# One decoder block with sixteen experts: a shorter routing step, a first expert gathered in quarters, and a norm row built later

## The chip, the cores and the metric

The kernel runs on one core of a Trainium2 chip. The metric is device time in microseconds (us) of one execution of the whole kernel. Lower is better.

## The reference, cut to what matters

256 tokens of width 2048 go through a mixing layer (8 attention heads, 8 gated recurrent heads, one output projection with a residual) and then through a mixture of experts: each token picks one of 4 groups and the 2 best of the 4 experts in it. All matrices are float32.

```python
x = x + jnp.concatenate([o_attn, o_rec], -1) @ w_out          # mixing layer
h2 = rms_norm(x, norm_ffn_g)
grp_w, grp_idx = lax.top_k(softmax(h2 @ w_grp + b_grp), 1)     # one group of 4
exp_logits = (h2 @ w_er[group] + b_er[group])                  # 4 experts in it
top_w, top_idx = lax.top_k(softmax(exp_logits), 2)             # two of them
combine = one_hot(4 * grp_idx + top_idx) * top_w / sum(top_w) * grp_w
for each expert e:
    hid = silu(h2 @ w_gate[e]) * (h2 @ w_up[e]) * combine[:, e]
    out = out + hid @ w_down[e]
return rms_norm(x + out, final_norm_g)
```

Each expert has 3 x 2048 x 1024 float32 weights, 25.2 MB. Sixteen of them are 403 MB and all are read.

## The kernel before

**Front half.** `proj_t` and `proj_n` run the projections on TensorE (PE). Weights come through two 1 MB buffers, are split into a high and a low part by ACT (L298) and DVE (L299) in units of half a buffer (`units`), and 24 matmuls per unit use them. After each unit `step(k)` lets the queue `bgq` of background generators go on by k steps. The last projection is by `w_out`, over two halves of its rows. The second half goes in five column blocks b = 0 to 4, the last two 256 wide (2 units each). After each block `out_block` adds to the residual `X` (= `x2`), squares it for the norm, transposes it, copies it to `xT` or `rd`, and adds its part of the router logits into `pl` (L679).

**Routing.** After `drain()` the logits `pl` are copied (L703), folded and turned to tokens on partitions by two matmuls into `plt` (L706), scaled by the row norm `r2` and biased into `Z` (L714). `first_max` finds the maximum of four and the first place that holds it, in five DVE operations. It runs for the best expert and the group together and again for the second expert. `selb` is the selection (L742). Five small matmuls (L744 to L748) give each token its rank in its expert, `rk`. `keep_busy` (L699) puts matmuls of no use into the gaps of PE.

**Experts.** Each expert takes up to 64 tokens (`CAP`). `gather_matrix` makes a 0/1 matrix `pg` scaled by `r2`. `gather` multiplies it with `x2` (16 matmuls of 512 columns, tile `pn`), ACT copies to `xn`, and `turn` transposes eight times and multiplies by the norm gain into `xg`, 16 chunks of 128 rows. For expert e, PE then runs in a fixed order (`mmo` and `transpose` keep program order): the gate product `ga` over four weight pieces, with `scatter` of expert e - 1 after the first piece, the up product `up` over four pieces, `gather` for e + 1, the transposes of `hid`, `turn` for e + 1, and the down product `pd` over four pieces. `gather` covers the time in which ACT and DVE make `hid`. At e = 1, after the third gate piece, `final_gain` builds a row of the last norm with 16 matmuls that have 16 rows.

**Weights of the experts.** All loads are issued by SP in one order. A piece is 2 MB. Pieces are numbered through: expert 0 has 0 to 11 (gate 0 to 3, up 4 to 7, down 8 to 11), expert 1 has 12 to 23, and so on. Pieces 0 to 10 are loaded before the experts start (0 in two halves, its second half last, into the buffer of the last split weights). The ring has nine buffers. From piece 21 on, piece p goes into the buffer of piece p - 9, so its load waits until PE has used that piece. Pieces 12 to 20 take over those of pieces 1 to 6 and 8 to 10, and the halves of 11 those of the halves of 0. So piece 22 (a down piece of expert 1) waits for 13 (a gate piece of expert 1), piece 24 (expert 2) for 15, and piece 29 for 20.

Of the kernel before, what the change touches and what calls it, by code (L numbers as in the profile page):

```python
# [9 lines left out]
F32 = mybir.dt.float32  # L10
# [9 lines left out]
P = 128  # L20
T = 256
NT = 2
# [15 lines left out]
def hybrid_block_kernel(  # L38
# [141 lines left out]
    rev = cst.tile([P, 4], F32, name="rev")  # L180
    nc.gpsimd.iota(rev, pattern=[[-1, 4]], base=4, channel_multiplier=0,
                   allow_small_or_imprecise_dtypes=True)

    ssq = cst.tile([P, NT, 5], F32, name="ssq")
    small8 = cst.tile([P, 8], F32, name="small8")
# [150 lines left out]
    def proj_n(aTh, aTl, c0=0, c1=NC, w=512):  # L336

        pp = pbig().rearrange("p (n f) -> p n f", n=2)[:, :, 0:w]
        c = c0
        while c < c1:  # L340
            for hi, lo in units():
                for k in range(1024 // w):
                    for n in range(NT):
                        ts = slice(n * P, (n + 1) * P)
                        ah, al = aTh[c // 8][:, c % 8, ts], aTl[c // 8][:, c % 8, ts]
                        mm(pp[:, n], ah, hi[:, k], start=c == c0, stop=False)  # L346
                        mm(pp[:, n], ah, lo[:, k], start=False, stop=False)  # L347
                        mm(pp[:, n], al, hi[:, k], start=False, stop=c == c1 - 1)  # L348
                    c += 1
                step(2 if c0 else 1)  # L350
        return pp


# [299 lines left out]
    pl = pm.tile([64, T], F32, name="pl")  # L653
    x2 = X

    def out_block(b, col, w, pp, last):
        bs = slice(col, col + w)
        for n in range(NT):
            V.tensor_tensor(x2[:, n, bs], x2[:, n, bs], pp[:, n], ALU.add)
            if last:  # L660
                jk = cst.tile([P, 512], BF16, name="jk", tag="jk", bufs=1)
                S.activation(jk[:, 0:w], x2[:, n, bs], AF.Square, accum_out=ssq[:, n, b:b + 1])
        yield
        if not last:
            return
        k = w // P
        for j in range(0, k, 2):
            xT = xTs[xi[0] % 2]
            xi[0] += 1
            pt = psmall().rearrange("p (j t) -> p j t", j=2)  # L670
            for i in range(2):
                for n in range(NT):
                    nc.tensor.transpose(
                        pt[:, i, n * P:(n + 1) * P],
                        x2[:, n, bs].rearrange("p (q j) -> p j q", j=k)[:, j + i], ident)
            V.tensor_copy(xT, pt)
            yield
            for i in range(2):
                mm(pl[32 * i:32 * i + 32], wr[:, col // P + j + i], xT[:, i],  # L679
                   start=b == 0 and j == 0, stop=b == 4)  # L680
            yield

    xTs = [cm.tile([P, 2, T], F32, name="xT"), rd]
# [1 line left out]
    for hf, blocks in ((0, half0), (1, half1)):  # L685
        for b, (col, w) in enumerate(blocks):
            pp = proj_n(oTh, oTl, 8 * hf, 8 * hf + 8, w)
            bgq.append(out_block(b, col, w, pp, hf == 1))
        if hf == 0:
            S.activation(rf[:, 0:1], rf[:, 0:1], AF.Sqrt)  # L690
    drain()
    while nxt < NEARLY:
        load()
# [2 lines left out]

    def keep_busy(k, ps, lhs, rhs):
        for i in range(k):
            mm(ps[0:lhs.shape[1], 0:P], lhs, rhs, start=True, stop=True)  # L699

    keep_busy(8, busy, ident, x2[:, 1, D - P:])
    lt = dist1[0:64]
    V.tensor_copy(lt, pl)  # L703
    plt = psmall()[:, :40].rearrange("p (n e) -> p n e", n=NT)
    for n in range(NT):
        mm(plt[:, n], lt[:, n * P:(n + 1) * P], fold[0:64], start=True, stop=True)  # L706


    r2 = small8[:, 2:4]
# [1 line left out]
    rstd(r2, r2, D)  # L711
    Z = cst.tile([P, 5, NT, 4], F32, name="Z")
    for n in range(NT):
        V.scalar_tensor_tensor(Z[:, :, n], plt[:, n].rearrange("p (g e) -> p g e", g=5),  # L714
                               r2[:, n:n + 1], bias.rearrange("p (g e) -> p g e", g=5),
                               ALU.mult, ALU.add)

    def first_max(dst, src, m, tmp, vm, k):

        V.tensor_reduce(m, src, AX.X, ALU.max)  # L720
        V.tensor_tensor(tmp, src, m.unsqueeze(2).to_broadcast([P, k, 4]), ALU.is_equal)
        V.tensor_tensor(tmp, tmp, rev.unsqueeze(1).to_broadcast([P, k, 4]), ALU.mult)
        V.tensor_reduce(vm, tmp, AX.X, ALU.max)
        V.tensor_tensor(dst, tmp, vm.unsqueeze(2).to_broadcast([P, k, 4]), ALU.is_equal)

    Zf = Z.rearrange("p g n e -> p (g n) e")
    ma = cst.tile([P, 10], F32, name="ma")
    mb = cst.tile([P, 8], F32, name="mb")
    vm = cst.tile([P, 10], F32, name="vm")
    tmp = cst.tile([P, 10, 4], F32, name="tmp")  # L730
    M1 = cst.tile([P, 10, 4], F32, name="M1")
    M2 = cst.tile([P, 8, 4], F32, name="M2")
    E2 = cst.tile([P, 8, 4], F32, name="E2")
    keep_busy(8, busy, Z.rearrange("p g n e -> p (g n e)"), ident)
    first_max(M1, Zf, ma, tmp, vm, 10)
    keep_busy(6, busy, M1.rearrange("p a e -> p (a e)"), ident)
    V.scalar_tensor_tensor(E2, M1[:, 0:8], -1e30, Zf[:, 0:8], ALU.mult, ALU.add)
    first_max(M2, E2, mb, tmp[:, 0:8], vm[:, 0:8], 8)
    V.tensor_tensor(M2, M2, M1[:, 0:8], ALU.add)
    gm = M1[:, 8:10].rearrange("p n g -> p g n").unsqueeze(3).to_broadcast([P, 4, NT, 4])  # L740
    selb = cst.tile([P, 4, NT, 4], BF16, name="selb")
    V.tensor_tensor(selb, M2.rearrange("p (g n) e -> p g n e", g=4), gm, ALU.mult)  # L742
    pr = psmall()[:, :48].rearrange("p (a g e) -> p a g e", a=3, g=4)
    mm(pr[:, 0], before, selb[:, :, 0], start=True, stop=True)  # L744
    mm(pr[:, 1], ones, selb[:, :, 0], start=True, stop=False)
    mm(pr[:, 1], before, selb[:, :, 1], start=False, stop=True)
    mm(pr[:, 2], ones, selb[:, :, 0], start=True, stop=False)
    mm(pr[:, 2], ones, selb[:, :, 1], start=False, stop=True)  # L748
# [6 lines left out]
    V.tensor_reduce(cmax, pr[:, 2].rearrange("p g e -> p (g e)"), AX.X, ALU.max)  # L755

# [5 lines left out]
    over = cst.tile([P, NT, 4, 4], F32, name="over")  # L762
    cmaxi = cst.tile([1, 1], I32, name="cmaxi")

    def weights_of_routes():
        V.tensor_tensor(Zf, Zf, ma.unsqueeze(2).to_broadcast([P, 10, 4]), ALU.subtract)
# [6 lines left out]
        V.tensor_tensor(tmp[:, 8:10], Zf[:, 8:10], M1[:, 8:10], ALU.mult)  # L773
# [9 lines left out]
        V.tensor_copy(cmaxi, cmax[:1])  # L783

    cm.release()
    pm.release()
    mp = tc.alloc_tile_pool(name="mp", bufs=1, side="right")
# [6 lines left out]
    def piece(e, kind, i):  # L794
        return loaded.pop((e * 3 + kind) * 4 + i)


    def mmo(*a, **k):
        tc.keep_in_program_order(mm(*a, **k))  # L799

    def transpose(dst, src):
        tc.keep_in_program_order(nc.tensor.transpose(dst, src, ident))  # L802

    def pscr():
        return pq.tile([P, 512], F32, name="pt", tag="pt", bufs=2)
# [25 lines left out]
    def turn(xn):  # L831

        xg = mp.tile([P, NC, CAP], F32, name="xg")
        for j in range(2):
# [4 lines left out]
            for z in range(2):  # L839
# [2 lines left out]
                                gfe[:, c0:c0 + 4].unsqueeze(2).to_broadcast([P, 4, CAP]),  # L842
                                ALU.mult)
        return xg

    def scatter_matrix(e):
        pcm = mp.tile([P, NT, P], F32, name="pcm")
# [49 lines left out]
            S.activation(gf[:, q * 512:(q + 1) * 512], ps.rearrange("p c f -> p (c f)"), AF.Copy)  # L897
        return gf

    xg = turn(gather(gather_matrix(0)))  # L900
    weights_of_routes()
    pend = None
    work = None
    for e in range(NE):
        ga = pq.tile([P, 512], F32, name="ga")
        up = pq.tile([P, 512], F32, name="up")
        for i in stream(ga, xg, e, 0):
            if i == 0 and pend is not None:
                if e == 1:
                    acc[1] = single(0, [P, D], name="acc1")  # L910
                scatter(*pend)
            if i == 2 and e == 1:
                gf = final_gain()
        for i in stream(up, xg, e, 1):
            if i == 1:
# [20 lines left out]
        if e + 1 < NE:  # L936
            xg = turn(xn)
        pd = ptwo("pd")
        if e < NE - 1:
# [160 lines left out]
```

## Time and profile before

| | |
|---|---|
| median of 3 runs | 1420.9 us (1419.77 to 1421.42) |
| the profiled execution | 1423.41 us, its span 1421.6 us |
| PE | 1324.4 us busy, 93% |
| DVE, ACT | 432.2 us, 275.1 us |
| read from memory | 480.54 MB |
| chain that ended last | PE 67%, DMA 29%, DVE 2%, ACT 1% |

The front half runs to about 480 us, the routing and the first gather to about 496 us, the experts to about 1409 us. The rows of the trace that are used below count from the start of the span. PE is TensorE's matmuls, DVE VectorE, ACT ScalarE, SPq the sequencer that issues DMAs. A granted clock of 1.00 is 2.4 GHz and 0.50 is 1.2 GHz.

### The profile page before, as it was taken

The numbers are of one execution on the slowest core, as the hardware profiler recorded it, in microseconds if no ns is written. First come the engines' busy times: TensorE is split into PE (matmuls) and PEld (weight loads), VectorE is DVE, ScalarE is ACT, GpSimd is POOL, SyncE is SP. The second block draws the span as 40 slices with busy tenths as digits, with TensorE's granted clock in tenths as the row PEclk, the third lists the DMA queues.
The fourth block names the chain that finished last, engine by engine and source line by source line (L and its number), as shares of the span: only waits on it lengthen the run. The fifth ranks groups of instructions, "written<-read, shape, count | busy, mean of one in ns | idle before, by whom it ended". The sixth has DMA issues, their size and how long they took to land.

```text
span 1421.6 us, 16461 instructions
## 1 busy us (share of the span) xinstructions
PE 1324.4 (93%) x7073; PEld 721.8 (51%) x7073; DVE 432.2 (30%) x646; ACT 275.1 (19%) x408; POOL 17.8 (1%) x47
## 2 busy tenths in 40 slices
PE   7999999999999999999999999898898988989885
PEld 7999898898887733333333323223232232322323
DVE  4554557557555411112112112111121111211112
ACT  5453543532533300000000000000000000000002
POOL 2000000000000000000000000000000000000002
PEclk9999999999999999999999999999999999999998
DMA  6555553554598598999999999999999999999995
GB/s 235 210 181 169 163 177 119 178 178 178 212 345 300 208 405 364 389 427 429 428 427 428 427 429 428 427 427 427 428 429 427 428 427 428 428 428 427 427 411 207
DMA packets 85437, 483.75 MB, mean 340 GB/s; under 512 B 16816, under 2 KB 19056, under 8 KB 60528
## 3 DMA queue, kind: packets, MB, share of 16 engines
q1 hardware_dynamic: 84704, 482.61, 84.1%
q8 instruction: 57, 0.93, 0.3%
q14 instruction: 20, 0.16, 0.0%
q10 hardware_dynamic: 656, 0.04, 0.0%
HBM read 480.54 MB, written 2.10 MB: 339 GB/s over the span
## 4 chain that ended last, share of the span: by engine, by line
PE 67%; DMA 29%; DVE 2%; ACT 1%; issue 1%; SPq 0%; ACTq 0%; DVEq 0%
DMA wt<-in_w_up_dram 25%; PE pd L799 12%; PE up L799 8%; PE ga L799 6%; PE pp L346 5%; PE pp L347 5%; PE pp L348 5%; PE pp L329 4%; PE pp L331 4%; PE pp L332 4%; PE pn L799 4%; DMA wt<-in_w_gate_dram 3%; PE pt L802 2%; PE pw L450 1%; PE psc L799 1%; DVE rest L935 1%
## 5 line engine op out<-in xcount | busy, mean ns | idle before, releaser
L799 PE MATMUL up<-wt,xg 128*64 128x512 f32 x1024 | 231.2, 597 | 38.8 <-DMA wt<-in_w_up_dram 38.8
L799 PE MATMUL ga<-wt,xg 128*64 128x512 f32 x1024 | 228.8, 599 | 4.2 <-DMA wt<-in_w_gate_dram 4.2
L799 PE MATMUL pd<-wt,rest 128*64 128x512 f32 (+1 forms) x1088 | 224.8, 569 | 2.8 <-ACT rest L984 2.0
L299 DVE TENSOR_TENSOR whl<-sh,whl 128x1024 fp32r<-128x1024 f32 x144 | 175.5, 1223 | 132.4 <-ACT whl L298 128.8
L298 ACT ACTIVATE whl<-sh 128x1024 fp32r<-128x1024 f32 x144 | 152.0, 1058 | 232.9 <-PE pp L348 107.6
L799 PEld LDWEIGHTS up<-wt,xg 128*64 128x64 f32 x1024 | 69.4, 137 | 188.5 <-issue 120.2
L799 PEld LDWEIGHTS ga<-wt,xg 128*64 128x64 f32 x1024 | 73.7, 138 | 155.1 <-issue 152.2
L329 PE MATMUL pp<-hTh,whl 128*128 128x256 f32 x512 | 147.4, 288 | 2.8 <-ACT hTh L364 2.6
L331 PE MATMUL pp<-hTl,whl 128*128 128x256 f32 x512 | 146.2, 285 | 0.9 <-DVE hTl L365 0.9
L799 PEld LDWEIGHTS pd<-wt,rest 128*64 128x64 f32 x1088 | 76.1, 137 | 139.5 <-issue 128.6
L332 PE MATMUL pp<-hTh,whl 128*128 128x256 f32 x512 | 145.9, 285 | 0.0
L869 DVE TENSOR_TENSOR rest<-rest,psc 128x1024 f32<-128x1024 f32 x28 | 34.2, 1221 | 254.6 <-PE psc L799 253.2
L329 PEld LDWEIGHTS pp<-hTh,whl 128*128 128x128 f32 x512 | 99.3, 194 | 3.8 <-ACT hTh L364 3.6
L331 PEld LDWEIGHTS pp<-hTl,whl 128*128 128x128 f32 x512 | 99.2, 194 | 1.5 <-DVE hTl L365 1.3
L332 PEld LDWEIGHTS pp<-hTh,whl 128*128 128x128 f32 x512 | 99.1, 194 | 0.0
L855 DVE COPY pT<-pt 128x256 f32<-128x256 f32 x16 | 6.8, 425 | 295.4 <-PE pt L802 295.4
L346 PE MATMUL pp<-whl,hTh 128*128 128x512 f32 x192 | 77.5, 404 | 0.0
L828 ACT ACTIVATE xn<-pn 128x512 f32<-128x512 f32 x32 | 19.1, 597 | 295.7 <-PE pn L799 295.7
L348 PE MATMUL pp<-whl,hTl 128*128 128x512 f32 x192 | 75.3, 392 | 0.0
L347 PE MATMUL pp<-whl,hTh 128*128 128x512 f32 x192 | 74.9, 390 | 0.0
L799 PE MATMUL pn<-X,pg 128*64 128x512 f32 x256 | 61.2, 599 | 12.8 <-ACT xn L828 12.1
L799 PE MATMUL psc<-rest,pT 64*128 64x512 f32 x240 | 63.7, 628 | 7.0 <-DVE rest L869 7.0
(273 smaller groups left out, 995.2 us busy)
## 6 DMA issues: line engine op xcount, KB each, us to landing
wt<-in_w_gate_dram SPq DMA_DIRECT2D x63, 2048.0 KB, 39.1
wt<-in_w_up_dram SPq DMA_DIRECT2D x60, 2048.0 KB, 34.9
wt<-in_w_down_dram SPq DMA_DIRECT2D x59, 2048.0 KB, 36.9
sh<-in_w_in_dram SPq DMA_DIRECT2D x55, 1024.0 KB, 5.1
sh<-in_w_out_dram SPq DMA_DIRECT2D x16, 1024.0 KB, 5.1
wt<-in_w_down_dram SPq DMA_DIRECT2D x8, 1024.0 KB, 14.2
wt<-in_w_up_dram SPq DMA_DIRECT2D x8, 1024.0 KB, 28.6
X<-in_x_dram SPq DMA_DIRECT2D x4, 512.0 KB, 7.1
```

What stands on the lines that cost most here:

```text
L298: S.activation(t[:, 0], raw[:, k * hf:k * hf + k], AF.Copy)
L299: V.tensor_tensor(t[:, 1], raw[:, k * hf:k * hf + k], t[:, 0].bitcast(F32), ALU.subtract)
L329: mm(o, hi[:, k, cs], ah, start=st and j % 2 == 0, stop=False, skip_group_check=True)
L331: mm(o, hi[:, k, cs], al, start=False, stop=False, skip_group_check=True)
L332: mm(o, lo[:, k, cs], ah, start=False, stop=sp, skip_group_check=True)
L346: mm(pp[:, n], ah, hi[:, k], start=c == c0, stop=False)
L347: mm(pp[:, n], ah, lo[:, k], start=False, stop=False)
L348: mm(pp[:, n], al, hi[:, k], start=False, stop=c == c1 - 1)
L799: tc.keep_in_program_order(mm(*a, **k))
L802: tc.keep_in_program_order(nc.tensor.transpose(dst, src, ident))
L828: S.activation(xn[:, j], ps[:, j], AF.Copy)
L869: V.tensor_tensor(acc[n][:, bs], x2[:, n, bs] if e == 0 else acc[n][:, bs], ps.rearrange("p z f -> p (z f)"), ALU.add)
```

## The change

- `step(4)` instead of `step(2)` after each unit of the two 256-wide blocks. Blocks 0 to 3 have their logits in `pl` by block 4's first unit; there `pl` is copied and folded into `plt`. Block 4 is transposed and copied for each half of the tokens, and its logits are added straight into `plt` by four small matmuls.
- The dummy square root that loads ACT's table stays in its place in the program (after the first half of `w_out`). The first `keep_busy(8)` goes.
- Both uses of `first_max` are replaced: two comparisons of each of four with each of four (128x160), a predicated copy, a sum, and two small operations give `selb`. The other two `keep_busy` (8 and 6) become one of 10. The maximum and the selection in full are made later, in `weights_of_routes`.
- Expert 0 is gathered by `gather_turned`: `x2` is the stationary operand and `pg` the moving one (64 columns), so that the result comes out transposed, a quarter (8 matmuls) at a time. The first quarter and half of the second precede the gate product; the rest of the second and the third stand after its first piece, together with `weights_of_routes`, and the fourth after its second piece.
- `gather` and `turn` for expert 1 stand after the down product of expert 0. For all other experts they stay.
- `final_gain` moves from e = 1 to e = 6.

```diff
-                step(2 if c0 else 1)
+                step(4 if w == 256 else 2 if c0 else 1)
...
+            if b == 4:
+                for n in range(NT):
+                    ts = slice(n * P, (n + 1) * P)
+                    for i in range(2):
+                        transpose(pt[:, i, ts], xj[:, n, j + i])
+                    V.tensor_copy(xT[:, :, ts], pt[:, :, ts])
+                for n in range(NT):
+                    for i in range(2):
+                        mmo(plt[0][:, n], xT[:, i, n * P:(n + 1) * P],
+                            wr[:, col // P + j + i, 0:20], start=False, stop=i == 1,
+                            skip_group_check=True)
+                return
...
+        if b == 3:
+            lt = dist1[0:64]
+            V.tensor_copy(lt, pl)
+            plt[0] = psmall()[:, :40].rearrange("p (n e) -> p n e", n=NT)
+            for n in range(NT):
+                mm(plt[0][:, n], lt[:, n * P:(n + 1) * P], fold[0:64], start=n == 0, stop=False,
+                   skip_group_check=True)
...
-            S.activation(rf[:, 0:1], rf[:, 0:1], AF.Sqrt)
+            tc.keep_in_program_order(S.activation(rf[:, 0:1], rf[:, 0:1], AF.Sqrt))
...
-    keep_busy(8, busy, ident, x2[:, 1, D - P:])
...
-    keep_busy(8, busy, Z.rearrange("p g n e -> p (g n e)"), ident)
-    first_max(M1, Zf, ma, tmp, vm, 10)
-    keep_busy(6, busy, M1.rearrange("p a e -> p (a e)"), ident)
-    V.scalar_tensor_tensor(E2, M1[:, 0:8], -1e30, Zf[:, 0:8], ALU.mult, ALU.add)
-    first_max(M2, E2, mb, tmp[:, 0:8], vm[:, 0:8], 8)
-    V.tensor_tensor(M2, M2, M1[:, 0:8], ALU.add)
+    keep_busy(10, busy, Z.rearrange("p g n e -> p (g n e)"), ident)
+    V.tensor_tensor(wins, zo, zs, ALU.is_gt)
+    V.tensor_tensor(ties, zo, zs, ALU.is_ge)
+    V.copy_predicated(wins, tri.unsqueeze(1).to_broadcast([P, 10, 4, 4]), ties)
+    V.tensor_reduce(rank, wins, AX.X, ALU.add)
+    V.tensor_scalar(G1n, rank[:, 8:10], 0.0, None, ALU.is_equal)
+    V.scalar_tensor_tensor(selb.rearrange("p g n e -> p (g n) e"), rank[:, 0:8], 2.0,
+                           G1.unsqueeze(2).to_broadcast([P, 8, 4]), ALU.is_lt, ALU.mult)
...
+    def gather_turned(xg, pg, b, q0, q1, pt):
+        xb = x2[:, :, b * 512:(b + 1) * 512].rearrange("t n (p q) -> t n q p", q=4)
+        for q in range(q0, q1):
+            for n in range(NT):
+                mmo(pt[:, q], xb[:, n, q], pg[:, n], start=n == 0, stop=n == 1)
+        if q1 == 4:
+            V.tensor_tensor(xg[:, 4 * b:4 * b + 4], pt,
+                            gfe[:, 4 * b:4 * b + 4].unsqueeze(2).to_broadcast([P, 4, CAP]),
+                            ALU.mult)
...
-    xg = turn(gather(gather_matrix(0)))
-    weights_of_routes()
+    gather_turned(xg, pg, 0, 0, 4, pturn())
+    pt1 = pturn()
+    gather_turned(xg, pg, 1, 0, 2, pt1)
...
         for i in stream(ga, xg, e, 0):
+            if e == 0 and i == 0:
+                gather_turned(xg, pg, 1, 2, 4, pt1)
+                gather_turned(xg, pg, 2, 0, 4, pturn())
+                weights_of_routes()
+            if e == 0 and i == 1:
+                gather_turned(xg, pg, 3, 0, 4, pturn())
...
-            if i == 2 and e == 1:
+            if i == 2 and e == 6:
                 gf = final_gain()
...
-        if e + 1 < NE:
+        if 0 < e < NE - 1:
             xn = gather(pg)
...
+        if e == 0:
+            xg = turn(gather(pg))
```

## Rows read from the trace of the kernel before

**Rows 1.** Page, part 2: GB/s moved by DMA, in 40 slices of 35.5 us.

```profile
GB/s 235 210 181 169 163 177 119 178 178 178 212 345 300 208 405 364 389 427 429 428 427 428 427 429 428 427 427 427 428 429 427 428 427 428 428 428 427 427 411 207
```

**Rows 2.** Chain that ended last, 768 to 830: start us, us, what.

```profile
814.98 34.48 DMA wt<-in_w_up_dram
```

**Rows 3.** Windows: us, busy (count) of PE, PEld, DVE, ACT, POOL; PEclk, DMA share, GB/s.

```profile
566.00:568.00 2.00, 2.00 (x8) 0.60 (x6) 0.00 (x0) 0.00 (x0) 0.00 (x0) 0.50 0.70 295
568.00:570.00 2.00, 2.00 (x10) 0.54 (x8) 0.00 (x0) 0.00 (x0) 0.00 (x0) 0.77 0.00 0
...
1384.00:1386.00 2.00, 0.75 (x4) 0.56 (x4) 1.16 (x2) 0.00 (x0) 0.00 (x0) 1.00 1.04 381
```

**Rows 4.** Timeline of SP: start us, us, engine, line, DMA issued.

```profile
479.93 0.42 SPq L260 DMA_DIRECT2D wt<-in_w_gate_dram  x1
...
556.04 0.33 SPq L267 DMA_DIRECT2D wt<-in_w_down_dram  x1
...
570.18 0.33 SPq L267 DMA_DIRECT2D wt<-in_w_gate_dram  x1
...
594.71 0.33 SPq L267 DMA_DIRECT2D wt<-in_w_up_dram  x1
```

**Rows 5.** DMA issues of 479.93, 556.04 and 594.71: KB each, us to landing.

```profile
wt<-in_w_gate_dram SPq DMA_DIRECT2D x1, 1024.0 KB, 12.1
...
wt<-in_w_down_dram SPq DMA_DIRECT2D x1, 2048.0 KB, 7.4
...
wt<-in_w_up_dram SPq DMA_DIRECT2D x1, 2048.0 KB, 8.5
```

**Rows 6.** Chain that ended last, 485 to 600: start us, us, what.

```profile
485.37 3.25 PE pp L699 x28
...
489.57 1.95 PE pn L799 x8
...
495.63 13.88 PE ga L799 x64
...
523.77 1.74 PE pn L799 x8
...
530.46 13.88 PE pd L799 x64
...
552.42 7.02 PE ga L799 x32
559.43 4.77 PE pt L799 x32
564.20 5.94 PE ga L799 x16
```

**Rows 7.** Timeline 468 to 500: start us, us, engine, line, op, out<-in, shapes.

```profile
472.27 0.75 PE L673 MATMUL pw<-ident,X 128*128 128x128 f32 x4
...
475.82 0.63 PE L679 MATMUL pl<-rd,wr 128*32 128x256 f32 x4
...
479.23 0.28 PE L348 MATMUL pp<-whl,oT 128*128 128x256 f32 x1
...
479.55 0.75 DVE L659 TENSOR_TENSOR X<-X,pp 128x256 f32<-128x256 f32 x2 [5.81 <-PE pp L348]
...
481.14 1.28 ACT L193 ACT_TABLE_LOAD   x1
...
484.20 0.62 PE L706 MATMUL pw<-fold,dist 64*128 64x20 f32 x4
484.93 0.38 DVE L714 SCALAR_TENSOR_TENSOR Z<-pw,small,bias 128x20 f32<-128x20 f32 x2 [1.50 <-PE pw L706]
```

**Rows 8.** Chain that ended last, 1370 to 1390: start us, us, what.

```profile
1381.82 1.96 PE up L799 x8
...
1386.15 3.70 PE pd L799 x32
```

**Rows 9.** Groups by form, 215 to 370: xcount | busy us, mean ns | idle before.

```profile
L450 PE MATMUL pw<-sg,sh 128*128 128x64 f32 x80 | 9.6, 272 | 0.0
```

More of the change, by code (lines that the diff above doesn't have):

```diff
@@ L179, in hybrid_block_kernel @@
                                 base=-32 * j, pattern=[[-1, 20]], channel_multiplier=1)
-    rev = cst.tile([P, 4], F32, name="rev")
-    nc.gpsimd.iota(rev, pattern=[[-1, 4]], base=4, channel_multiplier=0,
-                   allow_small_or_imprecise_dtypes=True)
+    trif = cst.tile([P, 4, 4], F32, name="trif")
+    nc.gpsimd.memset(trif, 1.0)
+    nc.gpsimd.affine_select(out=trif, in_=trif, compare_op=ALU.is_ge, fill=0.0, base=-1,
+                            pattern=[[1, 4], [-1, 4]], channel_multiplier=0)
+    tri = cst.tile([P, 4, 4], U8, name="tri")
+    nc.gpsimd.tensor_copy(tri, trif)
     ssq = cst.tile([P, NT, 5], F32, name="ssq")
@@ L654, in hybrid_block_kernel, with mmo, transpose @@
     x2 = X
+    def mmo(*a, **k):
+        tc.keep_in_program_order(mm(*a, **k))
+    def transpose(dst, src):
+        tc.keep_in_program_order(nc.tensor.transpose(dst, src, ident))
+    plt = [None]
     def out_block(b, col, w, pp, last):
@@ L670, in out_block @@
             pt = psmall().rearrange("p (j t) -> p j t", j=2)
+            xj = x2[:, :, bs].rearrange("p n (q j) -> p n j q", j=k)
+            if b == 4:
[10 more added lines that the diff above has]
+                return
             for i in range(2):
                 for n in range(NT):
-                    nc.tensor.transpose(
-                        pt[:, i, n * P:(n + 1) * P],
-                        x2[:, n, bs].rearrange("p (q j) -> p j q", j=k)[:, j + i], ident)
+                    nc.tensor.transpose(pt[:, i, n * P:(n + 1) * P], xj[:, n, j + i], ident)
             V.tensor_copy(xT, pt)
@@ L679, in out_block @@
                 mm(pl[32 * i:32 * i + 32], wr[:, col // P + j + i], xT[:, i],
-                   start=b == 0 and j == 0, stop=b == 4)
+                   start=b == 0 and j == 0, stop=b == 3)
+            yield
+        if b == 3:
[5 more added lines that the diff above has]
+                   skip_group_check=True)
             yield
@@ L698, in keep_busy @@
         for i in range(k):
-            mm(ps[0:lhs.shape[1], 0:P], lhs, rhs, start=True, stop=True)
-    keep_busy(8, busy, ident, x2[:, 1, D - P:])
[L702 to L706, printed above, removed]
+            mmo(ps[0:lhs.shape[1], 0:P], lhs, rhs, start=True, stop=True)
     r2 = small8[:, 2:4]
@@ L713, in hybrid_block_kernel @@
     for n in range(NT):
-        V.scalar_tensor_tensor(Z[:, :, n], plt[:, n].rearrange("p (g e) -> p g e", g=5),
+        V.scalar_tensor_tensor(Z[:, :, n], plt[0][:, n].rearrange("p (g e) -> p g e", g=5),
                                r2[:, n:n + 1], bias.rearrange("p (g e) -> p g e", g=5),
                                ALU.mult, ALU.add)
[L718 to L724, printed above, removed]
@@ L726, in hybrid_block_kernel @@
     Zf = Z.rearrange("p g n e -> p (g n) e")
     ma = cst.tile([P, 10], F32, name="ma")
-    mb = cst.tile([P, 8], F32, name="mb")
     vm = cst.tile([P, 10], F32, name="vm")
     tmp = cst.tile([P, 10, 4], F32, name="tmp")
-    M1 = cst.tile([P, 10, 4], F32, name="M1")
+    rank = cst.tile([P, 10, 4], F32, name="rank")
     M2 = cst.tile([P, 8, 4], F32, name="M2")
     E2 = cst.tile([P, 8, 4], F32, name="E2")
-    keep_busy(8, busy, Z.rearrange("p g n e -> p (g n e)"), ident)
-    first_max(M1, Zf, ma, tmp, vm, 10)
@@ L736, in hybrid_block_kernel @@
-    keep_busy(6, busy, M1.rearrange("p a e -> p (a e)"), ident)
-    V.scalar_tensor_tensor(E2, M1[:, 0:8], -1e30, Zf[:, 0:8], ALU.mult, ALU.add)
-    first_max(M2, E2, mb, tmp[:, 0:8], vm[:, 0:8], 8)
-    V.tensor_tensor(M2, M2, M1[:, 0:8], ALU.add)
-    gm = M1[:, 8:10].rearrange("p n g -> p g n").unsqueeze(3).to_broadcast([P, 4, NT, 4])
+    G1 = cst.tile([P, 8], F32, name="G1")
+    G1n = G1.rearrange("p (g n) -> p n g", n=NT)
+    keep_busy(10, busy, Z.rearrange("p g n e -> p (g n e)"), ident)
@@ new lines, in hybrid_block_kernel @@
+    wins = dist1[:, 0:160].rearrange("p (a b c) -> p a b c", a=10, b=4)
+    ties = xTs[0].rearrange("p j t -> p (j t)")[:, 0:160].rearrange("p (a b c) -> p a b c", a=10, b=4)
+    zo, zs = (Zf.unsqueeze(k).to_broadcast([P, 10, 4, 4]) for k in (2, 3))
+    V.tensor_tensor(wins, zo, zs, ALU.is_gt)
[3 more added lines that the diff above has]
+    V.tensor_scalar(G1n, rank[:, 8:10], 0.0, None, ALU.is_equal)
@@ L741, in hybrid_block_kernel @@
+    gm = G1.rearrange("p (g n) -> p g n", n=NT).unsqueeze(3).to_broadcast([P, 4, NT, 4])
     selb = cst.tile([P, 4, NT, 4], BF16, name="selb")
-    V.tensor_tensor(selb, M2.rearrange("p (g n) e -> p g n e", g=4), gm, ALU.mult)
+    V.scalar_tensor_tensor(selb.rearrange("p g n e -> p (g n) e"), rank[:, 0:8], 2.0,
+                           G1.unsqueeze(2).to_broadcast([P, 8, 4]), ALU.is_lt, ALU.mult)
     pr = psmall()[:, :48].rearrange("p (a g e) -> p a g e", a=3, g=4)
-    mm(pr[:, 0], before, selb[:, :, 0], start=True, stop=True)
@@ L745, in hybrid_block_kernel @@
[L745 to L748, printed above, removed]
+    mmo(pr[:, 0], before, selb[:, :, 0], start=True, stop=True)
+    mmo(pr[:, 1], ones, selb[:, :, 0], start=True, stop=False)
+    mmo(pr[:, 1], before, selb[:, :, 1], start=False, stop=True)
+    mmo(pr[:, 2], ones, selb[:, :, 0], start=True, stop=False)
@@ L749, in hybrid_block_kernel @@
+    mmo(pr[:, 2], ones, selb[:, :, 1], start=False, stop=True)
     rk = cst.tile([P, NT, 4, 4], F32, name="rk")
@@ L754, in hybrid_block_kernel @@
     cmax = cst.tile([P, 1], F32, name="cmax")
-    V.tensor_reduce(cmax, pr[:, 2].rearrange("p g e -> p (g e)"), AX.X, ALU.max)
     gs = small8[:, 4:6]
@@ L763, in hybrid_block_kernel, with cmax_of_ranks @@
     cmaxi = cst.tile([1, 1], I32, name="cmaxi")
+    def cmax_of_ranks():
+        V.tensor_reduce(cmax, pr[:, 2].rearrange("p g e -> p (g e)"), AX.X, ALU.max)
     def weights_of_routes():
+        V.tensor_reduce(ma, Zf, AX.X, ALU.max)
+        V.tensor_scalar(M2, rank[:, 0:8], 2.0, None, ALU.is_lt)
         V.tensor_tensor(Zf, Zf, ma.unsqueeze(2).to_broadcast([P, 10, 4]), ALU.subtract)
@@ L772, in weights_of_routes @@
         V.reciprocal(gs, gs)
-        V.tensor_tensor(tmp[:, 8:10], Zf[:, 8:10], M1[:, 8:10], ALU.mult)
+        V.tensor_tensor(tmp[:, 8:10], Zf[:, 8:10], G1n, ALU.mult)
         V.tensor_reduce(vm[:, 8:10], tmp[:, 8:10], AX.X, ALU.max)
@@ L783, in weights_of_routes @@
         V.tensor_copy(cmaxi, cmax[:1])
+    cmax_of_ranks()
     cm.release()
@@ L795, in piece @@
         return loaded.pop((e * 3 + kind) * 4 + i)
[L798 to L802, printed above, removed]
     def pscr():
@@ L898, in final_gain, with pturn @@
         return gf
-    xg = turn(gather(gather_matrix(0)))
-    weights_of_routes()
+    pg = gather_matrix(0)
+    xg = mp.tile([P, NC, CAP], F32, name="xg")
+    def pturn():
+        return pscr()[:, 0:256].rearrange("p (q s) -> p q s", q=4)
+    gather_turned(xg, pg, 0, 0, 4, pturn())
+    pt1 = pturn()
+    gather_turned(xg, pg, 1, 0, 2, pt1)
     pend = None
@@ L935, in hybrid_block_kernel @@
         V.tensor_copy(hT, pt)
-        if e + 1 < NE:
+        if 0 < e < NE - 1:
             xg = turn(xn)
```

## The prediction

> **What bounds the kernel now.** I read the page's second part first. From about 600 us on, DMA moves 427 to 429 GB/s in every slice until the last two, and between 490 and 600 it is lower [rows 1]. The chain of waits says the same: from 815 us on it runs through loads that need 34.48 us from issue to landing, seven transfers deep in a queue that never empties [rows 2]. A piece of 2.1 MB takes 2.1 / 0.428 = 4.9 us, an expert of twelve 58.9 us. So the end is set by the loads: it moves by as much as the load stream moves, and a us saved on PE counts only if it takes away a us in which DMA stood still. The windows show where it last stood still: at 568 it moves 0 GB/s [rows 3]. There SP waits for buffers. It issues piece 22 at 556.04 when PE is done with piece 13, piece 24 at 570.18 when PE is done with piece 15, and piece 29 at 594.71 after piece 20 [rows 4]. Piece 29 lands at 594.71 + 8.5 = 603.2 [rows 4, 5], and after it no pause is left. So the question is when piece 29 lands in the changed kernel.
>
> What delays 24 is the norm row of the last norm: 4.77 us, and then the fourth gate piece takes 5.94 us where two such pieces together took 7.02 [rows 6], because the clock had fallen to 0.50 [rows 3]. Together 4.77 + 5.94 - 3.47 = 7.2 us more PE time than a plain piece.
>
> **The change part by part.** I follow PE's chain from the end of the last projection, E, to the end of piece 13. Before, E is 479.51 [rows 7], the gate product of expert 0 starts at 495.63 [rows 6], and piece 13 is done at 555.9 (two pieces in the 7.02 us from 552.42) [rows 6].
>
> (1) Logits of block 3 inside block 4's projection. Its four transposes (0.75 us, some 0.5 of it without overlap), its logit matmuls (0.63) and the two that fold (0.62) [rows 7] now stand ahead of E, on a PE that has no gap there; with the changes of weights I take 2.0 us: E = 481.5. The other end: the logits wait for a copy, the fold for another, and if PE stands still for both and for the like wait in block 3, it is 2.2 us more, E = 483.7. I take the near end: the unit of block 4 that follows has 24 matmuls that wait for nothing and can fill these waits. The first rival takes the far end.
>
> (2) From E to Z. Before it is 5.8 us, from 479.51 to 484.93 + 0.38 = 485.31 [rows 7]. Now: the additions (0.75 us for two), of the second half of the tokens two transposes (0.4), a copy of 128x256 (0.4, as an addition of that size), two small matmuls (0.45), Z (0.38) [rows 7], and five handovers of 0.1: 2.9 us. ACT's table load of 1.28 us [rows 7] leaves the norm's chain, which is about as long. I take 3.1: Z at 484.6.
>
> (3) Counting. Six DVE operations: four on 160 elements, which cost at most the 0.38 of 256 [rows 7], and two small ones of 0.2, at most 2.1 us with handovers. Beside them stand ten useless matmuls, 20 of the records of which 28 took 3.25 us [rows 6]: 2.3 us. In program order these end last, so the saving of DVE is partly covered by the new filler: ranks at 487.0. Before they began when the fillers ended, at 485.37 + 3.25 = 488.62 [rows 6]. The predicated copy is not shown at this size; at the same price as the other three the filler ends 0.2 us after DVE, and if it took 0.5 us longer, 0.3 would be added. With less than the bound nothing is gained, since the filler is last.
>
> (4) Ranks to gather: 489.57 - 488.62 = 0.95 us [rows 6], unchanged. Gather at 487.9 (before 489.57).
>
> (5) First quarter and half of the second: 12 matmuls with 128x128 float32 weights and 64 columns. The nearest row is a matmul of that very form: 80 records (two for one matmul) in 9.6 us [rows 9], 0.24 each with the tail of each run in it. Within a run I take 0.217, an estimate from that. 2.6 us; the DVE multiplication of the first quarter lies beside the half. Gate product at 490.5, before 495.63: 5.1 us earlier. Its first piece needs the second half of piece 0. Before that lands at 479.93 + 12.1 = 492.0 [rows 4, 5]; it is issued behind E, so in the new kernel it is about 492.5, when it is needed (490.5 + 1.7 = 492.2). That caps this gain: were E not late at all, piece 0 would still end hardly 0.4 us sooner.
>
> (6) The other 2.5 quarters, 20 matmuls, now stand inside the gate product: 20 x 0.217 = 4.3 us later.
>
> (7) Gather for expert 1 behind the down product. Before, it hid the making of `hid`: 530.46 - 523.77 = 6.7 us from up to down [rows 6]. Uncovered, that step is shown at the last expert, which gathers nothing: 1386.15 - (1381.82 + 1.96) = 2.4 us [rows 8]. The gather alone then costs 495.63 - 489.57 = 6.1 us [rows 6]. 2.4 + 6.1 - 6.7 = 1.7 us later. The pause of DMA before piece 18 goes, but the same pause comes back before 21, since PE then gathers while no buffer is freed.
>
> Piece 13 is done 5.1 - 4.3 - 1.7 = -0.9, that is 0.9 us later: 556.8. `weights_of_routes` on DVE and ACT's table load for Exp lie under 14 us of gate product; some 20 small operations of 0.2 us and the load are about 6 us. Queued behind them on DVE is the fourth quarter's multiplication, which only the last gate piece waits for, some 9 us after they begin. No DMA issue changes its place in SP's order.
>
> (8) `final_gain` away from expert 1: pieces 14 and 15 follow at once, 15 is done at 563.7 (before 570.1), and 24 no longer waits. At e = 6 (from about 815 us) PE no longer runs ahead of the loads and waits for them. A buffer that comes free up to 7.2 us later is covered by the queue: of the 34.48 us to landing only 4.9 are the piece's own transfer [rows 2]. It costs nothing; without that cover 7.2.
>
> Sum: 22 issued at 557.0, lands at 557.0 + 7.4 [rows 5] = 564.4 (0.6 later if it takes as long as the others that start from rest), 29 seven transfers later at 564.4 + 34.3 = 598.7 to 599.3. Its own buffer is free at about 588, so it only queues. Before 603.2: 4.2 us, the middle of 3.9 and 4.5. The profiled execution of 1423.41 us (span 1421.6) becomes 1419.2. It lies 2.5 us above the median of 1420.9, so the median becomes 1416.7. Of the 4.2, moving `final_gain` gives some 5.1 and the rest of the change takes about 0.9.
>
> **A rule against this change.** Between E and Z PE has four transposes and four small matmuls instead of a filler that kept it busy. Before, in the stretch from 1384 to 1386 transposes were PE's only work, 0.75 of 2 us, and the clock stayed at 1.00 [rows 3]; it fell in the norm row's matmuls of 16 rows, and read 0.50 at 566 [rows 3]. "TensorE: Matmul & The Clock Gate" of the Trainium skill (Part 4: PE-mode transpose) says that transposes don't count as work for the clock gate and don't bring the high clock on. By that rule this stretch counts as nearly idle, and the second rival below would be likelier than its rows make it. The window at 1384 speaks against so strong a reading, but it is one short stretch. In numbers: 1416.7 by the row, 1424.2 by the rule in full.
>
> **The rivals.** *The inserted work costs more (0.26).* E at 483.7 (2.2 us), and 32 gather matmuls at 0.24 (0.7 us): 4.2 - 2.9 = 1.3 us, 1419.6, no change that can be told. For it: PE has no gap before E. Against: 24 matmuls of block 4 are ready to fill the waits.
>
> *The clock falls after E (0.10), slower.* At 1.2 GHz the fillers (2.3 us), the gathers ahead of the gate product (2.6) and its first piece (3.5) double, 8.4 us, less 0.9 that DVE and the late half of piece 0 would take anyway: piece 13 7.5 us later, 4.2 - 7.5 = -3.3, 1424.2. It decides from 7 us of delay on (4.2 + 2.8). Half of it gives no change. Against: the clock is at 1.00 through the routing and the uncovered `hid`; for: the fall in [rows 3], with PE busy throughout.
>
> *The edits do not act as I read them (0.04): the routing's 5.1 us count in full* because the quarters inside the gate product stand where PE would wait for loads. Then 4.2 + 4.3 = 8.5 us: 1412.4. Against: the last of the first loads, the late half of piece 0, lands at about 492 [rows 4, 5], and after it the gate product has no load to wait for.
>
> **How the numbers follow.** Forecast 1416.7, chance 0.60 (1415.9 to 1418). A measurement of this kernel can tell 0.2%, 2.8 us, from no change. Faster by more: 0.60 + 0.04 = 0.64. Within: 0.26. Slower: 0.10. The range leaves out the clock and the full gain: 1415.7, 1 us under the forecast (E not late, piece 22 landing in 7.4), to 1420.4, the first rival with 0.8 us for the spread of the runs before.
>
> **What would show it.** Right: 0.50 nowhere between 550 and 570; piece 22 issued within 1 us of 557; the gate product of expert 0 starting near 490.5; DMA without a pause from about 559 on; the norm row at e = 6 with DMA still at 428. Wrong in (1): the last projection ending after 483. Wrong in (5): quarters over 2 us. Wrong in (8): a dip in GB/s about e = 6. I would be wrong altogether if piece 22 were issued after 560, or if the loads paused again later.

## The result: 1435.8 us, slower by 1%

| | before | after |
|---|---|---|
| median | 1421.16 us (1419.77 to 1421.44) | 1435.78 us (1435.03 to 1436.12) |
| profiled execution, its span | 1423.41, 1421.6 | 1436.12, 1434.4 |
| piece 22 issued | 556.04 | 572.79 |
| piece 29 lands | 603.2 | 615.7 |

The ratio is 1.0099 (95% interval 1.0087 to 1.011). The forecast was 1416.7, so both the sign and the range were wrong.

Page of the kernel after, part 2: GB/s in 40 slices of 35.9 us.

```profile
GB/s 236 208 178 179 168 162 132 160 183 189 218 359 252 224 287 340 422 427 427 428 427 427 428 427 428 429 426 429 426 429 428 428 427 428 427 428 428 427 411 204
```

Beside [rows 1], the loads run at 426 to 429 from slice 18 on until the last two, so the bound is the same. What is late is the start of that stretch. SP's issues of pieces 22 and 24 (timeline of SP, kernel after; start us, us, engine, line, DMA):

```profile
572.79 0.33 SPq L271 DMA_DIRECT2D wt<-in_w_down_dram  x1
...
579.66 0.33 SPq L271 DMA_DIRECT2D wt<-in_w_gate_dram  x1
```

Piece 29 is issued at 604.18, takes 11.5 us and lands at 615.7. That is 12.5 us after the 603.2 of before, and the span is 12.8 us longer. The whole loss is therefore made before piece 22 goes out at 573 us. Where, the chain that ended last shows (kernel after; start us, us, what). It answers to [rows 6]:

```profile
481.06 0.13 PE pp L352
...
484.47 0.39 DVE Z L741 x2
484.90 4.06 PE pp L662 x20
...
489.91 5.83 PE pt L662 x24
495.74 5.05 PE ga L662 x16
500.79 5.79 PE pt L662 x24
506.58 4.75 PE ga L662 x16
511.33 3.88 PE pt L662 x16
515.21 8.71 PE ga L662 x32
523.92 6.87 PE up L662 x32
...
538.22 0.61 ACT rest L974
...
541.12 13.95 PE pd L662 x64
555.08 1.74 PE pn L662 x8
...
560.94 3.58 PE ga L662 x16
```

L662 is the helper that issues every matmul here, so the rows go by tiles: `pp` x20 is the filler behind Z, `pt` are the quarters of expert 0's gathering, `ga`, `up`, `pd` its products and `pn` the gathering for expert 1. Two things stand out. The 32 gather matmuls (64 records) take 5.83 + 5.79 + 3.88 = 15.5 us where 6.9 were forecast. And the four gate pieces between them take 18.51 us where before they took 13.88 [rows 6].

The forms of that stretch (kernel after, 484 to 516: shapes, count | busy us, mean ns of one | idle before) and its windows (us, busy of PE, PEld, DVE, ACT, POOL; PEclk, DMA share, GB/s):

```profile
L662 PE MATMUL pt<-pg,X 128*128 128x64 f32 x64 | 15.6, 413 | 0.7 <-DVE pg L838 0.7
L662 PEld LDWEIGHTS pt<-pg,X 128*128 128x128 f32 x64 | 15.2, 328 | 2.4 <-issue 1.6 <-PE pw L662 0.8
```

```profile
486.00:488.00 2.00, 2.00 (x11) 1.79 (x10) 0.64 (x4) 0.00 (x0) 0.00 (x0) 0.50 0.96 410
...
492.00:494.00 2.00, 2.00 (x10) 2.00 (x10) 0.09 (x1) 0.00 (x0) 0.00 (x0) 0.50 0.03 12
494.00:496.00 2.00, 2.00 (x10) 1.85 (x11) 1.86 (x13) 0.00 (x0) 0.00 (x0) 0.50 0.00 0
496.00:498.00 2.00, 2.00 (x6) 0.47 (x4) 0.21 (x1) 0.00 (x0) 0.00 (x0) 0.50 0.00 0
...
512.00:514.00 2.00, 2.00 (x10) 2.00 (x10) 0.00 (x0) 0.00 (x0) 0.00 (x0) 1.00 0.90 205
```

The row of 486 to 488 is the filler. In the two rows that hold quarters alone (492 and 512) PEld, the loading of weights, is busy all of the time (2.00 of 2.00). It is so at a clock of 0.50 and at 1.00, with the same ten records in 2 us: these rows speak for the load, and not the clock, as the price of the quarters. In gate windows the clock makes the difference: six records in 496 to 498 at 0.50, where at 1.00 sixteen take 3.58 us (row of 560.94), some nine in 2 us. GB/s is 0 from 494 to 498: SP has no free buffer to load into until PE is done with a piece.

### The profile page after: what moved, and what is told of

Same layout as the page of the kernel before. It is cut to its first block, busy times and chain, and to the rows that moved or that the text cites. A ratio compares the mean times of both kernels' runs of the same rounds, so it can differ in the third digit from the quotient of the medians.

```text
span 1434.4 us, 16494 instructions
## 1 busy us (share of the span) xinstructions
PE 1336.1 (93%) x7093; PEld 732.8 (51%) x7093; DVE 431.8 (30%) x642; ACT 274.0 (19%) x406; POOL 18.2 (1%) x49
## 4 chain that ended last, share of the span: by engine, by line
PE 68%; DMA 26%; DVE 2%; ACT 2%; issue 1%; SPq 0%; ACTq 0%; DVEq 0%
DMA wt<-in_w_up_dram 23%; PE pd L662 12%; PE up L662 9%; PE ga L662 7%; PE pp L350 5%; PE pp L351 5%; PE pp L352 5%; PE pp L333 4%; PE pp L335 4%; PE pp L336 4%; PE pn L662 4%; DMA wt<-in_w_gate_dram 3%; PE pt L665 2%; PE psc L662 1%; PE pt L662 1%; PE pw L454 1%
## 5 line engine op out<-in xcount | busy, mean ns | idle before, releaser
L662 PE MATMUL up<-wt,xg 128*64 128x512 f32 x1024 | 230.9, 597 | 36.0 <-DMA wt<-in_w_up_dram 36.0
L662 PE MATMUL ga<-wt,xg 128*64 128x512 f32 x1024 | 233.2, 608 | 4.4 <-DMA wt<-in_w_gate_dram 4.4
L662 PE MATMUL pd<-wt,rest 128*64 128x512 f32 (+1 forms) x1088 | 224.8, 569 | 3.5 <-ACT rest L1035 2.0
L662 PEld LDWEIGHTS up<-wt,xg 128*64 128x64 f32 x1024 | 69.5, 137 | 185.3 <-issue 121.7
L662 PEld LDWEIGHTS ga<-wt,xg 128*64 128x64 f32 x1024 | 74.0, 140 | 156.8 <-issue 152.7
L662 PEld LDWEIGHTS pd<-wt,rest 128*64 128x64 f32 x1088 | 76.1, 137 | 140.3 <-issue 128.6
L662 PE MATMUL psc<-rest,pT 64*128 64x512 f32 x240 | 63.7, 628 | 7.0 <-DVE rest L904 7.0
L662 PE MATMUL pn<-X,pg 128*64 128x512 f32 x240 | 57.4, 598 | 11.4 <-ACT xn L852 11.4
```

## Experiments

Two theories at the start. **Stride:** `gather_turned` reads `x2` as `(p q) -> q p`, so each 128x128 float32 stationary tile consists of every fourth column (16 bytes apart), and such a load takes twice as long. **Clock:** the routing with its gaps after E brings the clock down, and the quarters and pieces are slow for that. A third question is what each of the other parts (routing, norm row, expert 1's gathering) is worth.

### The quarters read from contiguous columns

```diff
-        xb = x2[:, :, b * 512:(b + 1) * 512].rearrange("t n (p q) -> t n q p", q=4)
+        xb = x2[:, :, b * 512:(b + 1) * 512].rearrange("t n (q p) -> t n q p", q=4)
...
+        if kind < 2 and e == 0:
+            return (w_gate, w_up)[kind][0, 0].rearrange("(c p) f -> p c f", p=P)[
+                :, 4 * i + a:4 * i + b, :]
```

The rows of expert 0's gate and up weights, and the norm gain, are loaded in the order that fits.

> The changed kernel, but expert 0's gathering reads x2 in plain runs of 128 columns instead of every fourth column, and its gate and up weights are loaded with the rows in that order (the result is the same). Theory A, the stride of the stationary operand sets the price: a record of the gather falls from 0.24 to about 0.12 us, the first 12 matmuls from 5.83 to about 2.9 us, 32 of them from 15.5 to 7.7; piece 22 is issued 8 us earlier and the time falls to about 1428, to 1423 if the clock's later falls go with it. Rival B, the shape (128x128 float32 weights for 64 columns) sets it: 5.8 us stay, 1436. Rival C, the clock sets it: 5.8 us where it is 0.50, 2.9 where it is 1.00.

Measured: 1425.48 us (1423.63 to 1427.2), ratio to before 1.0021 (1.0012 to 1.0031). Forms and chain of this kernel:

```profile
L665 PE MATMUL pt<-pg,X 128*128 128x64 f32 x64 | 7.8, 277 | 0.7 <-DVE pg L841 0.7
L665 PEld LDWEIGHTS pt<-pg,X 128*128 128x128 f32 x64 | 7.4, 192 | 2.4 <-issue 1.6 <-PE pw L665 0.8
```

```profile
485.79 2.39 PE pp L665 x20
...
489.13 2.86 PE pt L665 x24
491.99 3.58 PE ga L665 x16
495.58 2.82 PE pt L665 x24
498.40 3.58 PE ga L665 x16
501.98 1.93 PE pt L665 x16
503.91 7.02 PE ga L665 x32
...
528.13 15.62 PE pd L665 x64
```

The same 64 records take 7.6 us instead of 15.5, the mean load 192 ns instead of 328. With them goes the low clock in the gate product: its pieces take 14.18 us, near the 13.88 of before. The layout is the main cause: 10.3 us of the 14.6 lost. This row alone doesn't settle the pair of theories, since the filler ran at the full clock here too (2.39 us instead of 4.06), and expert 0's weights are read in another order. The next experiment and the one with PE kept busy tell the two apart.

### Every second column

```diff
-        xb = x2[:, :, b * 512:(b + 1) * 512].rearrange("t n (p q) -> t n q p", q=4)
+        xv = x2[:, :, b * 512:(b + 1) * 512].rearrange("t n (h p q) -> t n h q p", h=2, q=2)
...
-                mmo(pt[:, q], xb[:, n, q], pg[:, n], start=n == 0, stop=n == 1)
+                mmo(pt[:, q], xv[:, n, q // 2, q % 2], pg[:, n], start=n == 0, stop=n == 1)
```

Rows of `xg` meet the wrong rows of expert 0's weights here; the work is the same in kind and amount.

> The changed kernel with the quarters read at every second column (8 bytes) instead of every fourth (16 bytes); the rows are paired with the wrong weights, so that the output is not the reference's. If any stride costs: 0.24 us a record as with 4. If the cost goes with the bytes passed over: some 0.12 to 0.18 us.

Measured, one execution: 1427.45 us. Forms and two windows of this kernel:

```profile
L662 PE MATMUL pt<-pg,X 128*128 128x64 f32 x64 | 8.2, 283 | 0.7 <-DVE pg L838 0.7
L662 PEld LDWEIGHTS pt<-pg,X 128*128 128x128 f32 x64 | 7.8, 196 | 2.4 <-issue 1.6 <-PE pw L662 0.8
```

```profile
486.00:488.00 2.00, 2.00 (x11) 1.79 (x10) 0.55 (x4) 0.00 (x0) 0.00 (x0) 0.50 0.97 389
...
490.00:492.00 2.00, 2.00 (x19) 2.00 (x19) 0.26 (x3) 0.75 (x1) 0.00 (x0) 1.00 0.34 135
```

Columns 8 bytes apart cost nearly as little as contiguous ones (196 ns; the 64 records take 8.0 us); 16 bytes apart cost 328. So it is no steady growth with the stride. The weights are read in the order of the kernel after. The filler behind Z ran at 0.50 (4.00 us), as there, and yet the quarters took the short time and the gate product stayed at 1.00 (19 records in 490 to 492, against ten). That separates the two: a low clock before the quarters isn't what slows them, the stride of 16 bytes is.

### The changed kernel once more

> The changed kernel once more, for a second profile. Theory: the filler behind Z runs at the low clock in one execution and not in the next (4.0 against 2.4 us), since nothing in the program fixes it, while the gathering runs at 0.24 us a record and the clock falls inside it every time: 1434 to 1437. Rival: the filler is at the low clock always.

Measured, the kernel after unchanged, one more execution: 1436.73 us. Filler 3.93 us at 0.50, quarters 5.83, 5.79 and 3.88, gate pieces 5.37, 4.91 and 7.02. The quarters repeat to 0.01 us; the clock in the gate product falls in other places, and its total is 17.30 instead of 18.51. The down product of expert 0, at the full clock in the first profile (13.95), takes 15.65 here. That the filler would find another clock was a miss; the rival, the low clock always, fits these two profiles.

### PE kept busy between E and Z

```diff
+                fill = pbig()
+                keep_busy(2, fill, ident, ident)
                 for n in range(NT):
...
                     V.tensor_copy(xT[:, :, ts], pt[:, :, ts])
+                    keep_busy(2, fill, ident, ident)
```

> The changed kernel with six more matmuls of no use between the last projection and Z, two before and two after each half of the transposes. Theory A, the clock falls at 484 because of the gaps before Z, and later again because of the gathering itself: filler of 10 at 2.3 us instead of 4.06, later falls stay, 1434. Rival, the first fall carries the later ones: 1.00 all through, 1.7 + 4.7 us less, 1429.

Measured: 1437.17 us (1435.18 to 1437.97), ratio 1.0104 (1.0087 to 1.0121). Chain and a window of this kernel:

```profile
485.87 2.39 PE pp L662 x20
...
489.21 5.83 PE pt L662 x24
495.04 4.73 PE ga L662 x16
499.77 5.79 PE pt L662 x24
505.56 6.29 PE ga L662 x16
```

```profile
494.00:496.00 2.00, 2.00 (x9) 1.27 (x10) 1.33 (x8) 0.00 (x0) 0.00 (x0) 0.50 0.00 0
```

With the six useless matmuls the filler behind Z runs at the full clock (2.39 instead of 4.06). But the quarters stay at 5.83 and 5.79, and the clock falls all the same behind them. So the fall in the gate product comes with the slowly loaded quarters, not from the gaps after E; and as a whole nothing is gained (1434 was expected).

### The old gathering with the new routing

```diff
-    gather_turned(xg, pg, 0, 0, 4, pturn())
-    pt1 = pturn()
-    gather_turned(xg, pg, 1, 0, 2, pt1)
+    xg = turn(gather(gather_matrix(0)))
+    weights_of_routes()
...
-        if 0 < e < NE - 1:
+        if e + 1 < NE:
             xn = gather(pg)
```

The quarters inside the gate product go as well.

> The changed kernel with the gathering of the kernel before (512 columns, transposed afterwards, expert 1's beside hid), so only routing and norm row are changed. Theory A, the loss lies in the quarters: routing itself gains almost nothing since its filler runs at the low clock (ranks at 489 as before), so 1415.5 to 1417.5. Rival, the low clock that begins after the last projection goes on under any gathering and costs piece 0 and 1 some 3 us more: 1418 to 1421.

Measured: 1421.08 us (1418.81 to 1422.15), ratio 0.9992 (0.9983 to 1.0002). The new gathering alone (quarters, and expert 1's behind the down product) thus costs 14.7 us. What is left of the change, routing and norm row, comes out as no change that can be told, where 1415.5 to 1417.5 was expected. The norm row alone takes 1419.21 (below), so the new routing seems to take 1.9 us of that back and not to add to it; the two intervals just overlap, so this is likely and not settled.

### The same with PE kept busy

The edit of the old gathering and the two `keep_busy(2, fill, ident, ident)` of the one before it:

```diff
+    xg = turn(gather(gather_matrix(0)))
+    weights_of_routes()
...
+                    keep_busy(2, fill, ident, ident)
```

> Run e3 (changed routing and late norm row, old gathering) with six more matmuls of no use between the last projection and Z. Theory A: in most executions of e3 the clock falls after the last projection, as in the profile of the changed kernel, and costs some 2 us; with the gaps filled it stays, and the time is 1418 to 1419 with little spread. Rival B: e3 loses against e2 by the work that was put ahead of the last projection's end, not by the clock: 1421 as e3. Rival C: the filler itself delays the logits: 1422.

Measured: 1418.42 us (1417.97 to 1420.13), ratio 0.9981 (0.9972 to 0.999). It is narrower and lower than the last one, but the intervals overlap, and neither trace shows a fall of the clock between E and the gate product to explain it. The trace without fillers is that of its fastest execution. The mean granted clock of every execution is on record: 0.990 to 0.993 without the fillers, lowest (0.990) in the two slowest, and 0.995 to 0.996 with them. So the clock was lower without fillers; where it fell in the slower executions no trace shows, and that the fillers gain here is likely and not shown.

### The norm row alone

The kernel before with one line changed:

```diff
-            if i == 2 and e == 1:
+            if i == 2 and e == 6:
```

> The kernel before with the last norm's row built in expert 6 and nothing else changed. Theory: the pause of the loads at 568 goes, piece 24 is issued 7 us earlier, the end moves by the 5 us in which DMA stood still: 1415.8 to 1416.5. Rival: the row in expert 6 stops the loads there (7.2 us of PE where it waits for loads): 1421 to 1423.

Measured: 1419.21 us (1418.72 to 1420.77), ratio 0.9977 (0.9968 to 0.9987). A gain, but half of what was expected. SP's issues of pieces 24 to 27 in this kernel, as one group (timeline of SP):

```profile
563.09 11.15 SPq L267 DMA_DIRECT2D wt<-in_w_gate_dram  x4
```

Piece 24 goes out 7.1 us earlier than before (563.09, 570.18 [rows 4]), which is the 7.2 of the prediction. Piece 29 lands at 599.2 instead of 603.2, and the span falls by 3.9. Per execution the gain is only 2.5, because executions of before lie in two groups (15 of 25 from 1419.9 to 1422.1, ten from 1423.7 to 1424.6) and the profiled one, with its full fall of the clock behind the norm row, is near the upper. This kernel has no upper group. The mean granted clock on record fits a fall of the clock as the difference (0.993 to 0.994 in the upper group, 0.994 to 0.996 in the lower, 0.994 to 0.997 in this kernel). That it is the fall behind the norm row is only argued: no trace of an execution of the lower group was taken.

### Contiguous quarters, expert 1's gathering back beside `hid`

The first experiment and, on top of it:

```diff
-        if 0 < e < NE - 1:
+        if e + 1 < NE:
             xn = gather(pg)
...
-        if e == 0:
-            xg = turn(gather(pg))
```

> Run e1 (quarters in plain runs of columns) with expert 1's gathering back beside hid, as before the change. Theory: the move behind the down product costs 2.9 + 5.9 - 6.7 = 2.1 us of PE and, where the clock falls in the gap before pd (15.62 instead of 13.9 in e1), 1.7 more: 1422 to 1423.5 where e1 has 1425.5. Rival: the move pays since buffers come free sooner: above 1426.

Measured: 1422.61 us (1420.46 to 1425.15), ratio 1.0015 (1.0005 to 1.0024). The median is 2.9 us under that of the first experiment, but the intervals of the ratios overlap. There the clock fell in the down product, behind the wait for `hid` in which PE has little to do (window of that kernel, contiguous quarters):

```profile
529.00:531.00 2.00, 2.00 (x8) 0.71 (x6) 0.00 (x0) 0.00 (x0) 0.00 (x0) 0.50 1.07 459
```

Here the same product takes 13.88 us (chain of this kernel):

```profile
524.98 1.74 PE pn L665 x8
...
531.67 13.88 PE pd L665 x64
```

That is the fastest execution of ten (1420.46, the slowest took 1425.15). So the gathering beside `hid` can be worth more than its cover, since it also keeps PE at work; the kernel after had no fall in this product without it (13.95), so it is not so every time. The kernel is still slower than the norm row alone (1419.21). Its quarters take 2.86 + 2.82 + 1.93 = 7.6 us; the gathering of before takes 6.06 [rows 6].

### The scatter of expert 0 later

Two versions: the norm row alone, and the old gathering with the fillers, each with the scatter of expert 0 behind expert 1's last gate piece:

```diff
-            if i == 0 and pend is not None:
+            if i == (3 if e == 1 else 0) and pend is not None:
```

> Run e2 (before, with the norm row in expert 6) and expert 0's scatter after the fourth gate piece of expert 1 instead of after the first. Theory: piece 22 waits for piece 13, which is then done 4.6 us sooner, and the last pause of the loads (about 556) goes: 1 to 2 us less than e2's 1419.2, so 1417 to 1418.3. Rival: the pause only moves to a later piece, 1419.

> Run e5 (changed routing with its gaps filled, late norm row, old gathering) with expert 0's scatter after the fourth gate piece of expert 1, as in e7. Theory: both gains add, since both make piece 13 done sooner and only the pause before piece 22 is bounded: e7's 1417.8 less the 0.5 to 1 us of routing, 1416.8 to 1417.6. Rival: with the scatter late, no pause is left that the routing could shorten: 1417.8.

Measured: 1417.83 us (1416.98 to 1420.17), ratio 0.9979 (0.997 to 0.9988), and 1417.94 us (1416.19 to 1419.58), ratio 0.9967 (0.9954 to 0.9979). DMA's last pause closes: windows of the old gathering with fillers, then of the same with the late scatter (5 us each):

```profile
555.00:560.00 5.00, 5.00 (x26) 1.72 (x24) 0.00 (x0) 0.00 (x0) 0.00 (x0) 1.00 0.75 262
```

```profile
555.00:560.00 5.00, 4.54 (x22) 1.31 (x18) 2.11 (x2) 0.60 (x1) 0.00 (x0) 1.00 0.99 423
```

Both are faster than before. The second has the lowest ratio of the study, but its interval overlaps that of the first, and its median lies nearer to the rival of its expectation (1417.8, no pause left that the routing could shorten) than to both gains together (1416.8 to 1417.6). Against the versions without the late scatter (0.9977, 0.9981) the intervals overlap, so what the late scatter adds isn't settled by these runs.

## Why the prediction was wrong

The chain of PE in the kernel after, term by term up to the end of piece 13 (us):

| term | predicted | measured | late by |
|---|---|---|---|
| (1) E | 481.5 | 481.19 | -0.3 |
| (2) E to Z | 3.1 | 3.67 | 0.6 |
| (3) Z to ranks | 2.4 | 4.10 | 1.7 |
| (4) ranks to gather | 0.95 | 0.95 | 0 |
| (5) 12 gather matmuls | 2.6 | 5.83 | 3.2 |
| (6) 20 more | 4.3 | 9.67 | 5.4 |
| gate product itself | 13.88 | 18.51 | 4.6 |
| (7) up to down | 2.4 | 2.92 | 0.5 |
| the rest to piece 13 | | | 0.1 |
| piece 13 done | 556.8 | 572.65 | 15.9 |

**(1), (2), (4) and the shape of (7)** were right within 0.6 us. The near end of (1) was the right one: PE filled the waits of block 4. The `hid` step is 0.5 us longer than at the last expert since ACT's first operation on `rest` starts when the up product ends (538.22), and the gathering for expert 1 took 5.86 us where 6.1 were forecast. **(3)** came 1.7 us late by the clock of the filler (4.06 us where 2.3 were forecast), so that the gather starts at 489.91, later than the 489.57 of before: with the later E, the shorter routing gained nothing. The third rival, the routing's gain in full, is out: the quarters inside the gate product stand in the chain with their whole time, and PE waits for no load there.

**(5) and (6) failed**, for 8.6 us, and with them the gate product, for 4.6. The price of 0.217 us was taken from the row of the same form [rows 9]. That row's stationary operand is contiguous (`k[:, h, ts]`, 128 columns in a row), and the prediction didn't ask how the changed operand lies. The form of a row (128x64 by 128x128 float32) doesn't show the stride; only the code did, in the diff: `(p q) -> q p`. A matmul took 0.48 us (two records of 0.24). At 0.12 us a record the quarters come out at 7.6 us, near the 6.9 forecast and the 7.7 of the first rival; at 16 bytes' stride, 15.5. The signature that the prediction named for (5), quarters over 2 us, is what appeared: 5.83 us for one and a half.

**The gate product** was not in the sum at all. The second rival had a fall of the clock, between E and the first piece, for 7.5 us, and it named the mechanism; but its place and its cause were others. What fell there by itself was the filler, 1.7 us. Most came behind the slow quarters; with contiguous ones the clock is at 1.00 there.

**The rule against the change** was half right. PE's filler behind Z ran at 0.50 in three profiles with the new routing (kernel after, its repetition, stride 2) and at 1.00 in three others (contiguous quarters with expert 1's gathering in either place, and the old gathering), all with the same four transposes. In the three with extra fillers it took 2.39 us each time. "TensorE: Matmul & The Clock Gate" of the Trainium skill (Part 4: PE-mode transpose) says that transposes don't count as busy work for the clock gate. Three of these six traces agree and three don't, so the runs show a risk, and not that the transposes are its cause. In the three at 0.50 E came at 481.1 to 481.6, in the three at 1.00 at 481.9 to 482.1; whether that decides wasn't tried. The price of this fall was 1.7 us, not the 7.5 of the rival.

**(8) was right in the mechanism.** At e = 6 the row and the piece behind it cost PE 3.81 and 5.28 us (4.77 and 5.94 at e = 1 [rows 6]), the clock falls there as well, and the loads go on at 423 GB/s. Chain, then a window, of the kernel after:

```profile
842.93 3.81 PE pt L662 x32
846.74 5.28 PE ga L662 x16
```

```profile
845.00:850.00 5.00, 5.00 (x24) 2.47 (x24) 0.00 (x0) 1.73 (x3) 0.00 (x0) 0.68 0.99 423
```

Wrong was its size. First, from the landing of piece 22 to that of 29 it took 35.6 us in the kernel after and 35.7 in the one with the norm row alone, not 34.3 to 34.9: a gain of 3.9 in place of 5.1. Second, the profiled execution lies 2.5 us above the median, and the forecast both counted the fall of the clock as a gain and took the 2.5 off at the end. If that fall makes the upper group, it was counted twice; the measured gain against the median is 2.5.

Together: 1435.8 - 1416.7 = 19.1 us, of which 15.9 are the table, 0.7 to 1.3 the stream behind it, and the rest the step from the profiled execution to the median.

**Of the range:** its upper end came from a rival that priced the quarters at 0.24 us a matmul. The bound for an operand with another layout should have been open upwards. A row for a strided load was there, but it would not have warned: the transposes of `X`, most of them at every fourth column, the others at every second (kernel before, 440 to 485):

```profile
L673 PEld LDWEIGHTS pw<-ident,X 128*128 128x128 f32 x30 | 4.5, 206 | 1.7 <-PE pp L348 0.8 <-issue 0.4 <-DVE X L659 0.2
```

Their longest load is 220 ns. That the quarters' loads at the same stride take 328 was found only by trying.

## What to carry to other kernels

Before a matmul's price is taken from another row, compare how both stationary operands lie in memory, not only shape and type, and where they differ, try it; a view that "turns for free" may be paid in the load of weights, and the remedy may be to load what it meets later in an order that fits (here the rows of expert 0's weights). Work that seems to be only cover (a gathering beside `hid`) can also keep the clock up; ask what PE does in its place. And when the profiled execution is not the median one, ask which term of the sum makes the difference before taking it off again.

## What the runs showed of the hardware

- A 128x128 float32 stationary tile took 192 ns to load (mean) from contiguous columns, 196 from every second, 328 from every fourth; in a row of them the record costs 0.12, 0.13 and 0.24 us. In the last case its price was the same at a granted clock of 0.50 and 1.00.
- It isn't every load at that stride: most transposes of `X` in the projection read every fourth column too, and none of their loads took more than 220 ns (mean 206). What sets them apart wasn't tried.
- The granted clock fell to 0.50 with PE shown busy all the time: after slowly loaded quarters (494 to 498), and after the norm row's matmuls at e = 6 (0.68 from 845 to 850). It stayed at 1.00 at the norm row of e = 6 with the norm row alone, and with the old gathering and fillers. It also fell in the down product after an uncovered wait, in three of five profiles with expert 1's gathering behind that product (15.6 us instead of 13.9).
